# Summing the output's squares with a matrix of ones and taking the root for every column on GpSimd, in place of a root per token that is spread afterwards

## The chip, the core and the metric

The kernel runs on one core of a Trainium2 chip. The metric is the device time of one execution in microseconds (us); a kernel's time is the median of several runs. A profile of one further execution, taken by the hardware's own recorder, shows when each instruction ran. The engines are named as in the profile: PE is TensorE's matrix multiplication and PEld its loading of weights, DVE is VectorE, ACT is ScalarE, POOL is GpSimd, and SP is SyncE, which here only issues DMAs.

## The reference

One encoder layer is applied to 2,048 prompt tokens and 512 sample tokens of width 1,024 with shared weights. 16 learned meta tokens stand ahead of each sequence. The places that matter here are the last ones:

```python
y_a = (o_a * silu(za)) @ w_proj_a            # neighbourhood attention, gated
y_b = (o_b * silu(zb)) @ w_proj_b            # windowed attention, gated
h   = h + (sigmoid(ga) * y_a + sigmoid(gb) * y_b) @ w_out
out = h * rsqrt(mean(h * h, axis=-1) + 1e-6) * final_g      # the final RMSNorm
```

The final RMSNorm needs, for each token, the sum of squares over 1,024 features, its reciprocal root, and a product with all features of the token.

## The kernel before, in words

The 2,560 tokens are worked on in five windows of 512 (`NWIN`, `WTOK`), window 0 being the sample. Features lie on the 128 partitions and tokens along the free dimension, so that one row of features of a window is a tile of 128x512. All products run on pairs of tiles, a high part in `fp32r` and a low part that holds the rest of it, as three products (`mm3`, lines 146 to 148). The high part of a pair is a copy on ACT, the low part a subtraction; for weights (`wt`, `split_part`, lines 207 and 208) ACT copies and POOL subtracts, but for the last units of the last window, where `lo_eng` is DVE.

After the input projections, attention is cut into units: `unit_a` (neighbourhood) and `unit_b` (windowed), first all units "a" of a window, then all units "b". A hand-written loop interleaves the PE work of the units with a chain of generators called `dense`: at each place `fill` takes a few steps of it. PE's order is thus the order in which the code is written. ACT, DVE, POOL and, in this part, SP are ordered by a scheduler at build time; whatever order it chose, each engine and each queue then runs strictly in it.

For window w the dense chain is: `dense_pa(w)`, the product of `w_proj_a` with the gated output of branch a (PE tile `psa`, 8 rows of features, two steps each); `dense_pb(w)`, the same for branch b (`psb`); `dense_out(w)`, the product with `w_out` (`pso`). Those of neighbouring windows follow each other: units "b" of window w run beside the second half of `dense_out(w-1)` and `dense_pa(w)`, and units "a" of window w+1 beside `dense_pb(w)` and the first half of `dense_out(w)`.

`dense_out` leaves eight tiles `hT` (128x512, already multiplied by `final_g`), and POOL adds the squares of the features into one tile `ssq` (line 1372). `dense_fin(w-1)` runs in the steps of `dense_pa(w)` and closes window w-1. It sums `ssq` over the partitions by four products with a column of ones (`sums`, line 170: result `fin_v`, 128 tokens by 4), takes the reciprocal root of the 128x4 numbers on DVE (`rsqrt`, lines 153 to 163), puts them on diagonals (`diagonal`, line 177, tile `rs_dg`), spreads them to all partitions by four products with ones (`spread`, line 185, tile `rs_rb`), copies the result out of PSUM on ACT (`rbs`, line 1382), and multiplies the eight `hT` by it on POOL (line 1386). SP stores each. There are four such closings, of windows 0 to 3; the last window ends by other code (`finish_end`). They are called the first to the fourth closing here.

What else POOL does in that stretch matters: it makes the low parts of the weights (line 208), the gating product `y` of branch b (line 1280) and the low part `yb` of it (line 1072). The high part of `yb` is a copy on ACT (line 1071). `yb` has four parts, one for each pair of heads; the third and the fourth are made at the end of the units "b", and `dense_pb(w)` reads them as its third and fourth step of reduction for each row of features. In the fourth closing the third and fourth parts of `yb` are made on DVE instead.

PSUM tiles of the name `tp` (the transposes of probabilities, and `fin_v`, `rs_rb`) rotate over three banks.

Of the kernel before, what the change touches and what calls it, by code (L numbers as in the profile page):

```python
# [9 lines left out]
F32 = mybir.dt.float32  # L10
F32R = mybir.dt.float32r
I32 = mybir.dt.int32
AF = mybir.ActivationFunctionType
ALU = mybir.AluOpType
# [3 lines left out]
P = 128  # L18
D_MODEL = 1024
# [6 lines left out]
WTOK = 512  # L26
NWIN = TOK // WTOK
NEG = -1e30
EPS = 1e-6
# [66 lines left out]
def encoder_block(ctx: ExitStack, tc: tile.TileContext, xT, x_end, w_in, w_pa, w_pb, w_o, norm_g, final_g,  # L96
                  final_row, bias_a0, bias_a1, bias_a2, bias_a3, bias_b, bias_b0, outT_p, outT_s, out_e):
    nc = tc.nc
# [23 lines left out]
    def f32(ap):  # L122
        return ap.bitcast(F32)
# [17 lines left out]
    def move(out, in_):  # L141
        last_move[0] = nc.sync.dma_start(*(f32(a) if a.dtype == F32R else a for a in (out, in_)))
        return last_move[0]
# [6 lines left out]
    def rsqrt(small, sq, m, nc_):  # L150

        ve, hv, r, t = (small.tile([P, 8], F32, tag=f"rs{i}", name=f"rs{i}")[:m, :nc_] for i in range(4))
        nc.vector.tensor_scalar(ve, sq, 1.0 / D_MODEL, EPS, ALU.mult, ALU.add)
        nc.vector.tensor_scalar(r.bitcast(I32), ve.bitcast(I32), 1, None, ALU.arith_shift_right)
        nc.vector.tensor_scalar(r.bitcast(I32), r.bitcast(I32), -1.0, float(0x5F3759DF), ALU.mult, ALU.add)
        nc.vector.tensor_scalar(hv, ve, -0.5, None, ALU.mult)
        for _ in range(3):
            if nc_ == 1:
                nc.vector.scalar_tensor_tensor(t, r, hv, r, ALU.mult, ALU.mult)
            else:  # L160
                nc.vector.tensor_mul(t, r, hv)
                nc.vector.tensor_mul(t, t, r)
            nc.vector.scalar_tensor_tensor(r, t, 1.5, r, ALU.add, ALU.mult)
        return r

    def sums(ssq, c0, m, nc_, psum, tag):

        v = psum.tile([P, WTOK], F32, tag=tag, name="fin_v")
        for c in range(nc_):
            nc.tensor.matmul(v[:m, c : c + 1], ssq[:, c0 + c * m : c0 + (c + 1) * m], ones[:, 0:1],  # L170
                             start=True, stop=True)
        return v[:m, :nc_]

    def diagonal(dg, r, m, eng=nc.vector):

        nc_ = r.shape[1]
        eng.tensor_mul(dg[:m, : nc_ * m].rearrange("p (c n) -> p c n", n=m),
                             ident[:m, None, :m].broadcast_to([m, nc_, m]),
                             r[:m, :, None].broadcast_to([m, nc_, m]))

    def spread(psum, tag, dg, m, nc_):

        rb = psum.tile([P, WTOK], F32, tag=tag, name="rs_rb")
        for c in range(nc_):
            nc.tensor.matmul(rb[:, c * P : c * P + m], ones[:m, :], dg[:m, c * m : c * m + m], start=True, stop=True)
        return rb

    def by_ones(psum, tag, h, l, name):

        v = psum.tile([P, WTOK], F32, tag=tag, name=name)  # L190
        nc.tensor.matmul(v, ones_r, h, start=True, stop=False)
        nc.tensor.matmul(v, ones_r, l, start=False, stop=True)
        return v

    wpool = ctx.enter_context(tc.tile_pool(name="wpool", bufs=2))
    lo_eng, low = [nc.vector], [None]
# [1087 lines left out]
    pools = {}  # L1284
# [12 lines left out]
    acc = {}  # L1297
# [74 lines left out]
                nc.gpsimd.tensor_add(ssq, ssq, x)  # L1372

    def dense_fin(w):
        r = rsqrt(pools["d"], sums(acc["s", w], 0, P, 4, ps_p, "tp"), P, 4)
        dg = pools["d"].tile([P, WTOK], F32, tag="rbs", name="rs_dg", bufs=1)
        diagonal(dg, r, P)
        for _ in range(5):
            yield
        rb = spread(ps_p, "tp", dg, P, 4)  # L1380
        rbs = pools["d"].tile([P, WTOK], F32, tag="rbs", name="rbs", bufs=1)
        nc.scalar.copy(rbs, rb)
        for f in range(KT):
            hT = acc["h", w, f]
            with tc.issue_after(low[0]):
                nc.gpsimd.tensor_mul(hT, hT, rbs)
            dst = outT_s if w == 0 else outT_p
            c0 = 0 if w == 0 else (w - 1) * WTOK
            move(dst[f * P : (f + 1) * P, c0 : c0 + WTOK], hT)
            yield  # L1390
# [105 lines left out]
    def phases(w, br):  # L1496

        if br == "a":
            if w == 0:
                yield from islice(gates, GATES_A)  # L1500
            else:
                yield from dense_pb(w - 1)
                yield from dense_out(w - 1, range(0, 4))
        elif w == 0:
            yield from gates
            open_dense()
            yield from dense_pa(0)
        else:
            yield from dense_out(w - 1, range(4, 8))
            pa = dense_pa(w)  # L1510
            yield from islice(pa, 1)
            yield from with_fill(pa, dense_fin(w - 1))
# [8 lines left out]
    for w in range(NWIN):  # L1521
        for p in range(4):
            sh = {}
            units += [("a", w, unit_a(w, p, h, g, sh), 1) for h in range(2) for g in range(4)]
        for gh in range(2):
            sh = {}
# [15 lines left out]
    ps_p = ctx.enter_context(tc.tile_pool(name="ps_p", bufs=3, space=PSUM))  # L1542
# [9 lines left out]
    with tc.manual_schedule(engines={E.PE}):  # L1552
# [22 lines left out]
        for i in range(N):  # L1575
            br, w, _, weight = units[i]
# [128 lines left out]
```

## Time and profile before

| | |
|---|---|
| median of 3 runs | 1884.78 us (1884.11 to 1885.09) |
| profiled execution, its own time | 1881.95 us |
| its span, first to last instruction | 1880.0 us |
| granted TensorE clock | 0.998 |
| busy: PE, DVE, ACT, POOL | 1857.8, 1326.6, 1146.9, 729.4 us |

A row of the timeline reads: start in us from the span's start, duration in us, engine, line, operation, result<-operands, shapes and count; square brackets hold the idle time of the engine just before and what ended it. Consecutive instructions of one kind are merged into one row with their count. PE overlaps matrix products, so that the pitch, the distance between two starts, is what a product takes up and not its duration. A row of the groups ends in busy time, mean duration in ns, and idle time before.

### The profile page before, as it was taken

How to read it: one execution, taken by the hardware profiler on the slowest of the kernel's cores; microseconds unless marked ns; L12 is line 12 of the kernel's file. 1: busy time of each engine (PE TensorE's matmuls, PEld its weight loads, DVE VectorE, ACT ScalarE, POOL GpSimd, SP SyncE). 2: the span in 40 equal slices, each digit the busy share in tenths (PEclk: the TensorE clock that was granted, in tenths of full speed). 3: DMA queues.
4: the chain of work that ended last, by engine and by line, in shares of the span. 5: the costliest groups of instructions: out<-in, count | busy, mean ns of one | idle time of the engine just before them, and what ended most of it. 6: DMA issues, size and time to landing. Idle time of an engine off the chain costs nothing.

```text
span 1880.0 us, 29819 instructions
## 1 busy us (share of the span) xinstructions
PE 1857.8 (99%) x9797; PEld 1584.9 (84%) x9797; DVE 1326.6 (71%) x2961; ACT 1146.9 (61%) x2528; POOL 729.4 (39%) x558
## 2 busy tenths in 40 slices
PE   8999999999999999999999999999999999999998
PEld 6988888888888888888878888888888888888887
DVE  8885657556477565444457888878887887888874
ACT  6454444434465443444456797797889788878932
POOL 2005343222202322232323435656844764684420
PEclk9999999999999999999999999999999999999999
DMA  7575666555295677744359878977995996698473
GB/s 262 193 197 187 189 188 183 200 193 184 78 330 197 188 209 208 201 145 150 113 186 320 270 230 264 300 218 243 324 284 178 321 315 225 221 314 261 115 298 132
DMA packets 288145, 414.35 MB, mean 220 GB/s; under 512 B 117736, under 2 KB 162360, under 8 KB 286456
## 3 DMA queue, kind: packets, MB, share of 16 engines
q1 hardware_dynamic: 287704, 412.45, 68.4%
q8 instruction: 78, 1.28, 0.3%
q14 instruction: 75, 0.61, 0.1%
q10 hardware_dynamic: 288, 0.01, 0.0%
HBM read 303.46 MB, written 108.91 MB: 219 GB/s over the span
## 4 chain that ended last, share of the span: by engine, by line
PE 83%; ACT 5%; DVE 5%; DMA 4%; issue 1%; SPq 1%; POOL 1%; ACTq 0%; DVEq 0%
PE pa L850 23%; PE pe L850 11%; PE pc L850 6%; PE mm L148 3%; PE mm L147 3%; PE mm L146 3%; PE tp L1141 3%; PE pso L148 2%; PE psb L148 2%; PE pso L146 2%; PE psb L146 2%; PE pso L147 2%; PE psb L147 2%; PE psa L146 2%; PE psa L148 2%; PE psa L147 2%
## 5 line engine op out<-in xcount | busy, mean ns | idle before, releaser
L208 POOL TENSOR_TENSOR wt<-wraw,wt 128x512 fp32r<-128x512 f32 x164 | 213.0, 1317 | 270.0 <-ACT wt L207 269.9
L850 PE MATMUL pa<-u,wt 128*128 128x512 f32 x1008 | 244.3, 391 | 2.1 <-ACT wt L207 1.1
L850 PE MATMUL pa<-u,x 128*128 128x512 f32 x984 | 236.7, 389 | 0.5 <-ACT u L861 0.5
L850 PEld LDWEIGHTS pa<-u,wt 128*128 128x128 f32 x1008 | 189.9, 189 | 42.4 <-ACT wt L207 1.5
L207 ACT CAST wt<-wraw 128x512 fp32r<-128x512 f32 x312 | 177.9, 619 | 74.7 <-DMA wraw<-in_w_in_dram 27.4
L850 PEld LDWEIGHTS pa<-u,x 128*128 128x128 f32 x984 | 184.5, 188 | 39.3 <-ACT u L861 0.9
L821 POOL TENSOR_TENSOR s<-wraw,raw 128x512 f32<-128x512 f32 x40 | 58.2, 1456 | 278.8 <-DVE x L208 278.8
L146 PE MATMUL mm<-u,wt 128*128 128x512 f32 (+2 forms) x416 | 150.3, 361 | 7.0 <-ACT u L334 7.0
L816 POOL TENSOR_TENSOR s<-raw 128x512 f32<-128x512 f32 x40 | 58.7, 1467 | 234.7 <-DMA raw<-in_w_in_dram 233.2
L147 PE MATMUL mm<-u,wt 128*128 128x512 f32 (+2 forms) x416 | 146.8, 353 | 1.1 <-DVE u L335 1.0
L148 PE MATMUL mm<-u,wt 128*128 128x512 f32 (+2 forms) x416 | 146.8, 353 | 0.1
L208 DVE TENSOR_TENSOR wt<-wraw,wt 128x512 fp32r<-128x512 f32 x148 | 104.7, 745 | 53.8 <-ACT wt L207 53.7
L850 PE MATMUL pe<-u,wt 128*128 128x512 f32 x504 | 121.4, 390 | 0.0
L850 PE MATMUL pc<-u,wt 128*128 128x512 f32 x504 | 121.1, 389 | 0.0
L850 PE MATMUL pe<-u,x 128*128 128x512 f32 x480 | 115.3, 389 | 0.0
L850 PEld LDWEIGHTS pc<-u,wt 128*128 128x128 f32 x504 | 94.6, 188 | 19.6
L850 PEld LDWEIGHTS pe<-u,wt 128*128 128x128 f32 x504 | 94.4, 188 | 19.6
L1144 ACT CAST ph<-tp 128x384 fp32r<-128x384 f32 (+6 forms) x160 | 81.7, 511 | 44.9 <-PE tp L1141 43.5
L1047 DVE CUSTOM_DVE_ANT_0 s<-s,ba 128x384 f32<-128x384 f32 (+5 forms) x160 | 86.9, 544 | 30.6 <-PE s L1118 27.7
L1145 DVE TENSOR_TENSOR pl<-tp,ph 128x384 fp32r<-128x384 f32 (+6 forms) x160 | 94.9, 593 | 18.0 <-ACT ph L1144 15.2
L146 PE MATMUL pso<-mh,wt 128*128 128x512 f32 x256 | 107.1, 418 | 0.0
L829 POOL TENSOR_TENSOR s<-wraw,s 128x512 f32<-128x512 f32 x40 | 53.7, 1343 | 136.2 <-DVE wt L208 135.6
(258 smaller groups left out, 5030.1 us busy)
## 6 DMA issues: line engine op xcount, KB each, us to landing
wraw<-in_w_in_dram SPq DMA_DIRECT2D x86, 512.0 KB
raw<-in_w_in_dram SPq DMA_DIRECT2D x40, 512.0 KB
q<-qa SPq DMA_DIRECT2D x40, 512.0 KB
wraw<-in_w_o_dram SPq DMA_DIRECT2D x32, 512.0 KB
kbt<-kb SPq DMA_DIRECT2D x32, 384.0 KB
qa<-evq SPq DMA_DIRECT2D x20, 512.0 KB
qb<-evq SPq DMA_DIRECT2D x20, 512.0 KB
ka<-evk SPq DMA_DIRECT2D x20, 512.0 KB
```

Of the source, the lines that this page charges most:

```text
L146: nc.tensor.matmul(ps, wh, uh, start=first, stop=False)
L147: nc.tensor.matmul(ps, wh, ul, start=False, stop=False)
L148: nc.tensor.matmul(ps, wl, uh, start=False, stop=last)
L207: nc.scalar.copy(h, r)
L208: low[0] = (eng or lo_eng[0]).tensor_sub(l, r, f32(h)).ins
L816: eng.tensor_add(s1, a21, a22)
L821: eng.tensor_sub(s3, a11, a21)
L850: nc.tensor.matmul(ps, wt[:, a, s], u[:, b, kk, :], start=first and kk == 0 and i == 0, stop=kk == 3 and i == 2, skip_group_check=True)
L1047: nc.vector.tensor_tensor_reduce(s[:, :n], s[:, :n], bias, -1.0, 3.0e38, ALU.add, ALU.min, nm)
L1141: nc.tensor.transpose(tp[:kb, i * P : (i + 1) * P], pr[:, x : x + kb], ident)
L1144: nc.scalar.copy(ph_[:kb, a], tb)
L1145: nc.vector.tensor_sub(pl_[:kb, a], tb, f32(ph_[:kb, a]))
```

## The change

The sum over partitions is made for all 512 tokens at once and arrives on all 128 partitions. `ssq` is cut into a high part `ssh` (ACT) and a low part `ssl` (POOL), and two products of a 128x128 matrix of ones with them (`by_ones`, lines 191 and 192) give `fin_v`, 128x512, in which all partitions hold the same numbers. ACT copies it out of PSUM with scale and epsilon (`ve`), DVE makes a first guess of the reciprocal root from the bits in one instruction, and POOL takes three Newton steps of four instructions each on the full 128x512 tile. Nothing is put on a diagonal and nothing is spread. The tiles lie in the buffers of the low parts `ml` that are free at that time.

```diff
     def dense_fin(w):
-        r = rsqrt(pools["d"], sums(acc["s", w], 0, P, 4, ps_p, "tp"), P, 4)
-        dg = pools["d"].tile([P, WTOK], F32, tag="rbs", name="rs_dg", bufs=1)
-        diagonal(dg, r, P)
-        for _ in range(5):
+        ssq = acc["s", w]
+
+        def spare(i, dtype, name):
+            return pools["m"].tile([P, WTOK], dtype, tag=f"ml{i}", name=name)
+
+        sh, sl = (spare(i, F32R, f"ss{x}") for i, x in enumerate("hl"))
+        nc.scalar.copy(sh, ssq)
+        nc.gpsimd.tensor_sub(sl, ssq, f32(sh))
+        for _ in range(2):
             yield
-        rb = spread(ps_p, "tp", dg, P, 4)
-        rbs = pools["d"].tile([P, WTOK], F32, tag="rbs", name="rbs", bufs=1)
-        nc.scalar.copy(rbs, rb)
+        v = by_ones(ps_p, "tp", sh, sl, "fin_v")
+        ve, r, t = (spare(i, F32, name) for i, name in ((2, "ve"), (3, "rbs"), (4, "rt")))
+        nc.scalar.activation(ve, v, AF.Copy, bias=EPS, scale=1.0 / D_MODEL)
+        nc.vector.tensor_scalar(r.bitcast(I32), ve.bitcast(I32), -0.5, float(0x5F3759DF), ALU.mult, ALU.add)
+        for _ in range(3):
+            with tc.issue_after(low[0]):
+                nc.gpsimd.tensor_mul(t, r, ve)
+                nc.gpsimd.tensor_mul(t, t, r)
+                nc.gpsimd.tensor_scalar(t, t, -0.5, 1.5, ALU.mult, ALU.add)
+                nc.gpsimd.tensor_mul(r, r, t)
+            yield
         for f in range(KT):
             hT = acc["h", w, f]
             with tc.issue_after(low[0]):
-                nc.gpsimd.tensor_mul(hT, hT, rbs)
+                nc.gpsimd.tensor_mul(hT, hT, r)
```

`issue_after(low[0])` keeps an instruction behind the latest low part of weights in POOL's order. The scheduler's order moves with the change. On PE the first closing's sums stand behind a unit's transposes; before:

```order
L1243 MATMUL tp<-ident,prs 128x128 x6
L1246 MATMUL tp<-ident,prs 32x128
L170 MATMUL fin_v<-ones,ssq 128x1 x4
L146 MATMUL psa<-ya_11187,wt 128x512
L147 MATMUL psa<-ya_11188,wt 128x512
```

and now, one unit later:

```order
L1243 MATMUL tp<-ident,prs 128x128 x6
L1246 MATMUL tp<-ident,prs 32x128
L191 MATMUL fin_v<-ssh,ones 128x512
L192 MATMUL fin_v<-ssl,ones 128x512
L146 MATMUL psa<-ya_11187,wt 128x512
```

The sums moved behind the transposes of the next unit; the four products of line 185 are gone, and no other row of PE moved.

POOL, first closing, from the first `hT` on; `y_12477` and `y_12552` are the gating products of the third and fourth part of `yb_12614`. Before:

```order
L1386 TENSOR_TENSOR hT<-hT,rbs 128x512 x2
L208 TENSOR_TENSOR wt<-wraw,wt 128x512 x2
L1386 TENSOR_TENSOR hT<-hT,rbs 128x512 x4
L1280 TENSOR_TENSOR y_12477<-y_12477,z 128x512
L208 TENSOR_TENSOR wt<-wraw,wt 128x512 x2
L1386 TENSOR_TENSOR hT<-hT,rbs 128x512 x2
L1072 TENSOR_TENSOR yb_12614<-y_12477,yb_12613 128x512
L1280 TENSOR_TENSOR y_12552<-y_12552,z 128x512
L1072 TENSOR_TENSOR yb_12614<-y_12552,yb_12613 128x512
L208 TENSOR_TENSOR wt<-wraw,wt 128x512 x2
```

The same place now, from the third instruction of the second Newton step on (six instructions of the steps and two of line 208 stand ahead of these rows):

```order
L1393 TENSOR_SCALAR rt<-rt 128x512
L1394 TENSOR_TENSOR rbs<-rbs,rt 128x512
L1391 TENSOR_TENSOR rt<-rbs,ve 128x512
L1392 TENSOR_TENSOR rt<-rt,rbs 128x512
L1393 TENSOR_SCALAR rt<-rt 128x512
L1280 TENSOR_TENSOR y_12477<-y_12477,z 128x512
L1394 TENSOR_TENSOR rbs<-rbs,rt 128x512
L208 TENSOR_TENSOR wt<-wraw,wt 128x512 x2
L1399 TENSOR_TENSOR hT<-hT,rbs 128x512 x4
L1072 TENSOR_TENSOR yb_12614<-y_12477,yb_12613 128x512
L1399 TENSOR_TENSOR hT<-hT,rbs 128x512 x4
L1280 TENSOR_TENSOR y_12552<-y_12552,z 128x512
```

behind which come two of line 208 and then the last `yb_12614`. The gating product of the fourth part of `yb` now stands behind all Newton steps and all eight `hT`, and its low part behind two low parts of weights as well.

The second closing has the same order. In the third, POOL's end is:

```order
L1280 TENSOR_TENSOR y_17195<-y_17195,z 128x512
L1394 TENSOR_TENSOR rbs<-rbs,rt 128x512
L208 TENSOR_TENSOR wt<-wraw,wt 128x512 x2
L1072 TENSOR_TENSOR yb_17332<-y_17195,yb_17331 128x512
L1280 TENSOR_TENSOR y_17270<-y_17270,z 128x512
L1399 TENSOR_TENSOR hT<-hT,rbs 128x512 x8
L1072 TENSOR_TENSOR yb_17332<-y_17270,yb_17331 128x512
L208 TENSOR_TENSOR wt<-wraw,wt 128x512 x2
```

Here the gating product moved ahead of the `hT`, and only its low part, `yb`, stands behind all eight.

## The prediction

> **What bounds the kernel now.** I read the page's first part, then PE's waits in the last 680 us, where the closings lie, then the timelines of PE and POOL around each closing. The first row is from the page, the others are the whole answer on who made PE wait from 1200 us on (total, times, longest).
>
> ```profile
> PE 1857.8 (99%) x9797; PEld 1584.9 (84%) x9797; DVE 1326.6 (71%) x2961; ACT 1146.9 (61%) x2528; POOL 729.4 (39%) x558
> PE fin_v L170 <- DVE pms L1261: 0.5, 2, 0.3
> PE ob L1267 <- DVE y L1277: 0.5, 1, 0.5
> PE s L1223 <- DMA kbt<-kbm: 0.4, 1, 0.4
> PE fin_v L170 <- POOL ssq L1372: 0.3, 1, 0.3
> ```
>
> PE is the bound: it waits 1.7 us in 680. What leaves PE's order is gained, and any wait put into it is paid in full, since no idle time later can take it up. POOL's 39% is a mean; what counts is its queue in the closings.
>
> **What PE loses and gets.** First closing, PE's timeline: the sums, and the same passage one unit later without them.
>
> ```profile
> 1277.99 0.27 PE L1246 MATMUL tp<-ident,prs 128*32 128x128 f32 x1
> 1278.53 1.05 PE L170 MATMUL fin_v<-ones,ssq 128*128 128x1 f32 x8 [0.26 <-POOL ssq L1372]
> 1279.44 0.48 PE L146 MATMUL psa<-ya,wt 128*128 128x512 f32 x1
> 1279.76 0.40 PE L147 MATMUL psa<-ya,wt 128*128 128x512 f32 x1
> 1279.99 0.39 PE L148 MATMUL psa<-ya,wt 128*128 128x512 f32 x1
> ...
> 1284.49 0.27 PE L1246 MATMUL tp<-ident,prs 128*32 128x128 f32 x1
> 1284.52 0.49 PE L146 MATMUL psa<-ya,wt 128*128 128x512 f32 x1
> ```
>
> Without sums the next product starts 0.03 us after the transpose, with them 1.45 us after it: they cost 1.42. The fourth closing, where PE did not wait for them, and its spreading:
>
> ```profile
> 1778.04 0.27 PE L1246 MATMUL tp<-ident,prs 128*32 128x128 f32 x1
> ...
> 1779.24 0.48 PE L146 MATMUL psa<-ya,wt 128*128 128x512 f32 x1
> ...
> 1790.55 1.05 PE L185 MATMUL rs_rb<-rs_dg,ones 128*128 128x128 f32 x8
> 1791.36 0.48 PE L146 MATMUL psa<-ya,wt 128*128 128x512 f32 x1
> ```
>
> Sums 1.20 - 0.03 = 1.17; spreading 0.81. The four sums lie between 4 x 1.17 = 4.7 and 4 x 1.42 = 5.7; three of them had a wait of about 0.3, so I take 5.4. Spreading is 4 x 0.81 = 3.2. Added are two 128x512 products per closing at the pitch of lines 147 to 148 above, 0.23: 4 x 0.46 = 1.8. PE gains 5.4 + 3.2 - 1.8 = 6.8 us; up to the end of one of the first three closings it is ahead by 1.42 + 0.81 - 0.46 = 1.8.
>
> **What POOL gets.** Thirteen instructions on 128x512 per closing: `ssl`, nine two-input products and three of one input. First closing, before:
>
> ```profile
> 1284.73 2.54 POOL L208 TENSOR_TENSOR wt<-wraw,wt 128x512 fp32r<-128x512 f32 x2 [6.26 <-ACT wt L207]
> ...
> 1296.01 2.55 POOL L1386 TENSOR_TENSOR hT<-hT,rbs 128x512 f32<-128x512 f32 x2 [8.73 <-ACT rbs L1382]
> ...
> 1301.01 5.05 POOL L1386 TENSOR_TENSOR hT<-hT,rbs 128x512 f32<-128x512 f32 x4
> 1306.02 1.29 POOL L1280 TENSOR_TENSOR y<-y,z 128x512 f32<-128x512 f32 x1
> ...
> 1313.53 1.29 POOL L1280 TENSOR_TENSOR y<-y,z 128x512 f32<-128x512 f32 x1
> 1315.60 1.29 POOL L1072 TENSOR_TENSOR yb<-y,yb 128x512 fp32r<-128x512 f32 x1 [0.78 <-ACT yb L1071]
> 1316.84 2.55 POOL L208 TENSOR_TENSOR wt<-wraw,wt 128x512 fp32r<-128x512 f32 x2
> ```
>
> Idle for 6.26 and 8.73 us, then full. The last `yb` is done at 1316.9. PE's step that reads it is the fourth step of the first row of `dense_pb`; its second product (line 147) has the low part as operand:
>
> ```profile
> 1319.47 0.40 PE L146 MATMUL psb<-yb,wt 128*128 128x512 f32 x1
> 1319.71 0.39 PE L147 MATMUL psb<-yb,wt 128*128 128x512 f32 x1
> ```
>
> So `yb` had 2.8 us to spare, and PE will come 1.8 us earlier. Now this `yb` stands behind the whole of the Newton steps and the eight `hT`. Queued behind the slow POOL are ACT (the high part of `yb` needs the gating product) and PE.
>
> *Prices.* Mean of all `hT`, the only one-input instruction of this size, and two dependent POOL instructions at another place:
>
> ```profile
> L1386 POOL TENSOR_TENSOR hT<-hT,rbs 128x512 f32<-128x512 f32 x32 | 42.7, 1361 | 33.5 <-ACT rbs L1382 33.5
> L1370 POOL COPY ssq<-xres 128x512 f32<-128x512 f32 x4 | 2.5, 613 | 0.0
> 282.24 1.28 POOL L816 TENSOR_TENSOR s<-raw 128x512 f32<-128x512 f32 x1
> 283.60 1.62 POOL L817 TENSOR_TENSOR s<-s,wraw 128x512 f32<-128x512 f32 x1
> ```
>
> Independent two-input ones follow each other at (5.05 - 1.29) / 3 = 1.25 us at best and last 1.36 in the mean; I take 1.30. Dependent ones, as in a Newton step, came 283.60 - 282.24 = 1.36 apart; I take that, with 1.25 (the wait costs nothing) and 1.47 (1.36 and the mean's 0.11 more) as ends. The one-input TENSOR_SCALAR stands nowhere on POOL: at least the copy's 0.61, at most a two-input one's 1.47; nearest is the copy with one dependent wait of 0.11, 0.72. The Newton steps are 9 x 1.36 + 3 x 0.72 = 14.4 us (13.1 to 17.6).
>
> [...]
>
> *When the steps start.* The first guess needs PE's sums, then ACT and DVE. The transpose of 1284.49 comes at 1283.1; the two products end by 1283.8. ACT first does a unit's casts:
>
> ```profile
> 1285.65 0.86 ACT L1250 CAST ph<-tp 128x512 fp32r<-128x512 f32 x2
> 1295.35 0.58 ACT L1382 COPY rbs<-rs_rb 128x512 f32<-128x512 f32 x1
> ```
>
> If they move up with PE they end at about 1285.1, `ve` costs what `rbs` did, 0.6, and the guess on DVE about as much: 1286.4. POOL is free of line 208 by then (1287.3 - 1.4). For the second and third closing I take the end of that line's pair, less 1.4 (first and third row below: 1455.2 and 1622.2). A us earlier is the other end.
>
> ```profile
> 1453.49 3.09 POOL L208 TENSOR_TENSOR wt<-wraw,wt 128x512 fp32r<-128x512 f32 x2 [7.46 <-ACT wt L207]
> 1487.36 0.39 PE L147 MATMUL psb<-yb,wt 128*128 128x512 f32 x1
> 1620.50 3.09 POOL L208 TENSOR_TENSOR wt<-wraw,wt 128x512 fp32r<-128x512 f32 x2 [7.47 <-ACT wt L207]
> 1653.68 0.40 PE L147 MATMUL psb<-yb,wt 128*128 128x512 f32 x1
> ```
>
> *The sum.* From the start to the last `yb` POOL does, in the first two closings, the steps and 18 other two-input instructions: six low parts of weights, two gating products, two `yb`, eight `hT`. 14.4 + 18 x 1.30 = 37.8 (35.6 to 42.1). In the third the last two low parts come later: 16, and 35.2 (33.1 to 39.4). `yb` is ready at 1324.2, 1493.0 and 1657.4, where PE read it at 1319.7, 1487.4 and 1653.7. The difference is the net delay of the closing, PE's gain already inside, as it waits there anyway: +4.5 (1.3 to 8.8), +5.6 (2.4 to 9.9), +3.7 (0.6 to 7.9).
>
> Fourth closing: no `yb` on POOL, so the gain stays, -1.17 - 0.81 + 0.46 = -1.5. POOL's `hT` end later, and so do SP's stores, with loads of the tail behind them; DVE's two-input instructions are stretched while POOL runs:
>
> ```profile
> 1792.30 12.29 POOL L1386 TENSOR_TENSOR hT<-hT,rbs 128x512 f32<-128x512 f32 x8 [14.03 <-ACT rbs L1382]
> 1793.73 3.37 DVE L208 TENSOR_TENSOR wt<-wraw,wt 128x512 fp32r<-128x512 f32 x2
> 1815.66 0.92 SPq L142 DMA_DIRECT2D sgb<-gb  x2
> ```
>
> Steps from about 1786.5, 14.4 + 8 x 1.3: the `hT` end at 1811 instead of 1804.6, before the loads of 1815.66, which stand behind the last stores. For DVE's stretching I add 0.5 (0 to 3.5): -1.0 (-1.5 to +2.0).
>
> Costed at nothing: ACT's one more 128x512 instruction per closing (0.6), covered as PE waits for POOL afterwards; DVE's 13 small instructions and the diagonal, off PE's path. In the first closing the loads behind the stores of `hT` were issued about here:
>
> ```profile
> 1320.80 0.64 SPq L142 DMA_DIRECT2D q<-qa  x1
> ```
>
> The eighth `hT` ends at 1286.4 + 14.4 + 14 x 1.3 = 1319.0, so those loads keep their place, if barely.
>
> Total: 4.5 + 5.6 + 3.7 - 1.0 = +12.8 us (2.8 to 28.6) on the profiled execution, 1881.95 us, which lies 2.8 below the median of the runs. On that median, 1884.78: 1897.6 us, between 1887.6 and 1913.4.
>
> **The rivals.**
> - *`yb` comes in time* (faster). Then all of PE's gain stands: 1884.8 - 6.8 = 1878.0. From 1286.4 to where PE will read, 1319.7 - 1.8 = 1317.9, POOL has 31.5 us for 30 instructions, 1.05 each. It decides at that price; the two-input ones, 27 of the 30, never took under 1.25.
> - *Gain and wait cancel*: net delays below 1.3 us per closing, 1881 to 1888.6. It takes the lower ends of all prices and an early start.
> - *Longer still*: one-input instructions dearer than two-input ones, or DVE holding POOL up: beyond 28.6, over 1913. The copy's row speaks against the first.
> - *DVE held up rather than PE waiting for POOL.* DVE's normalisations of units "b" last 0.43 us, at worst 1.57:
>
> ```profile
> L1065 DVE TENSOR_SCALAR prs<-prs,rd x64: 360/431/1565, 1219.1 to 1784.5; 128x402 f32<-128x402 f32 x56, 128x274 f32<-128x274 f32 x8
> ```
>
> Three such DVE instructions per closing, each held 1.1 us, are 3.3 x 4 = 13.2 us less the 6.8: 1891. That wants `yb` in time as well, as the two waits overlap. [...]
>
> **How the numbers follow.** `yb` late by the prices above 0.68, longer still 0.07, DVE held up 0.05, cancelled 0.10, in time 0.10. A measurement of this kernel tells about 0.2%, 3.8 us, from no change. Slower is 0.68 + 0.07 + 0.05 = 0.80, same 0.10, faster 0.10. I predict the main case, 1898 us. The range 1886 to 1911 leaves out the faster case, half of the cancelled one and the longer one's far end.
>
> **What would show it.** Right: in the first three closings PE's waits name the third or fourth part of `yb` or its ACT copy at `psb`, some 4 to 9 us each, POOL has no gap from the first guess to the last `yb`, lines 191 and 192 pitch at 0.23. Wrong: `psb` starts without a wait; POOL's Newton steps take under 12 us; PE waits at `fin_v` for `ssl`, or at `tp`.

## The result, and the profile after

The changed kernel takes 1902.81 us (median of 5 runs, 1901.39 to 1904.55), the kernel before, measured beside it, 1884.11 (1883.30 to 1885.09): a ratio of 1.0101, 95% interval 1.0089 to 1.0113. It is slower by 1.0%, or 18.7 us. The prediction said slower, 1898 us, with a range of 1886 to 1911.

The profiled execution of the changed kernel has a span of 1900.6 us against 1880.0. The page's first part shows that PE is busy as before and that POOL has 61 us more:

```profile
PE 1859.1 (98%) x9741; PEld 1584.6 (83%) x9741; DVE 1321.1 (70%) x2909; ACT 1149.9 (60%) x2532; POOL 790.7 (42%) x610
```

What made PE wait from 1200 us on; where 1.7 us stood before, there are now 20.8:

```profile
PE psb L147 <- POOL yb L1072: 9.6, 3, 4.8
PE psb L146 <- ACT yb L1071: 7.7, 2, 3.9
PE pse L1459 <- DVE sgb L1444: 2.2, 1, 2.2
PE psb L146 <- DVE sgb L1444: 1.1, 1, 1.1
...
```

The three waits for POOL's `yb` and the two for ACT's copy of it lie in the first three closings. POOL's timeline in the first closing shows why. From the first Newton instruction to the last `yb` it has no gap, and the gating product of the fourth part (line 1280) comes only after all eight `hT`:

```profile
1286.00 1.28 POOL L1391 TENSOR_TENSOR rt<-rbs,ve 128x512 f32<-128x512 f32 x1 [1.57 <-DVE rbs L1388]
1287.37 1.30 POOL L1392 TENSOR_TENSOR rt<-rt,rbs 128x512 f32<-128x512 f32 x1
...
1306.54 5.04 POOL L1399 TENSOR_TENSOR hT<-hT,rbs 128x512 f32<-128x512 f32 x4
...
1312.77 5.01 POOL L1399 TENSOR_TENSOR hT<-hT,rbs 128x512 f32<-128x512 f32 x4
1317.72 1.28 POOL L1280 TENSOR_TENSOR y<-y,z 128x512 f32<-128x512 f32 x1
...
1321.39 1.28 POOL L1072 TENSOR_TENSOR yb<-y,yb 128x512 fp32r<-128x512 f32 x1
```

PE at the same place: the new products with ones, then the two waits, and behind them something that the prediction did not have. Line 148 used to start 0.23 us after line 147; here products of this size follow each other at about 0.43:

```profile
1281.18 0.27 PE L1246 MATMUL tp<-ident,prs 128*32 128x128 f32 x1
1281.27 0.47 PE L191 MATMUL fin_v<-ssh,ones 128*128 128x512 f32 x1
1281.58 0.40 PE L192 MATMUL fin_v<-ssl,ones 128*128 128x512 f32 x1
1281.81 0.40 PE L146 MATMUL psa<-ya,wt 128*128 128x512 f32 x1
...
1319.70 0.79 PE L146 MATMUL psb<-yb,wt 128*128 128x512 f32 x1 [3.85 <-ACT yb L1071]
1322.72 0.80 PE L147 MATMUL psb<-yb,wt 128*128 128x512 f32 x1 [2.23 <-POOL yb L1072]
...
1326.73 0.63 PE L147 MATMUL psb<-yb,wt 128*128 128x512 f32 x1
1327.16 0.63 PE L148 MATMUL psb<-yb,wt 128*128 128x512 f32 x1
```

The table of windows names the reason. A row holds a stretch and its length, the busy time and number of instructions of PE, PEld, DVE, ACT and POOL, and then the granted clock, the DMA share and GB/s. The clock falls to half at 1318.05, while PE waits, and comes back at 1328.29, 5.6 us after PE has its operand:

```profile
1314.64:1318.05 3.41, 1.21 (x8) 0.74 (x6) 2.56 (x8) 1.16 (x3) 3.41 (x4) 1.00 1.08 326
1318.05:1321.47 3.42, 0.79 (x1) 0.29 (x1) 0.00 (x0) 0.62 (x1) 3.42 (x4) 0.50 1.03 306
...
1324.88:1328.29 3.41, 3.41 (x11) 2.72 (x11) 1.48 (x4) 2.00 (x5) 2.42 (x2) 0.50 1.01 396
1328.29:1331.71 3.42, 3.42 (x22) 2.94 (x22) 1.67 (x5) 1.85 (x5) 0.00 (x0) 1.00 0.64 236
```

The other two closings look alike:

```profile
1497.21 0.79 PE L147 MATMUL psb<-yb,wt 128*128 128x512 f32 x1 [2.52 <-POOL yb L1072]
...
1668.99 0.79 PE L147 MATMUL psb<-yb,wt 128*128 128x512 f32 x1 [4.82 <-POOL yb L1072]
```

To see where the time went, one product is followed through both traces: the first `psa` of each `dense_pa`, which stands just ahead of each closing. Before, for the second to fourth closing, and a transpose behind the fourth:

```profile
1440.60 0.48 PE L146 MATMUL psa<-ya,wt 128*128 128x512 f32 x1
1607.60 0.48 PE L146 MATMUL psa<-ya,wt 128*128 128x512 f32 x1
1773.18 0.49 PE L146 MATMUL psa<-ya,wt 128*128 128x512 f32 x1
1793.27 0.27 PE L1246 MATMUL tp<-ident,prs 128*32 128x128 f32 x1
```

and after:

```profile
1445.47 0.48 PE L146 MATMUL psa<-ya,wt 128*128 128x512 f32 x1
1619.77 0.48 PE L146 MATMUL psa<-ya,wt 128*128 128x512 f32 x1
1790.45 0.49 PE L146 MATMUL psa<-ya,wt 128*128 128x512 f32 x1
1809.04 0.27 PE L1246 MATMUL tp<-ident,prs 128*32 128x128 f32 x1
```

The delay is 4.87, 12.17, 17.27 and 15.77 us at these places. At the landmark ahead of the first closing (1273.14 and 1271.27) it is -1.87, by which the one execution happens to be ahead; in the experiments below this product lies anywhere between 1270.3 and 1274.0. So the first three closings cost 6.7, 7.3 and 5.1 us, the fourth gains 1.5, and from there to the end of the span another 4.8 us are lost (20.6 - 15.8).

### The profile page after: what moved, and what is told of

It is laid out like the page before. It is cut to its first block, busy times and chain, and to the rows that moved or that the text cites. A ratio compares the mean times of both kernels' runs of the same rounds, so it can differ in the third digit from the quotient of the medians.

```text
span 1900.6 us, 29716 instructions
## 1 busy us (share of the span) xinstructions
PE 1859.1 (98%) x9741; PEld 1584.6 (83%) x9741; DVE 1321.1 (70%) x2909; ACT 1149.9 (60%) x2532; POOL 790.7 (42%) x610
## 3 DMA queue, kind: packets, MB, share of 16 engines
q8 instruction: 78, 1.28, 0.3%
## 4 chain that ended last, share of the span: by engine, by line
PE 75%; ACT 5%; POOL 4%; DVE 4%; DMA 3%; issue 2%; SPq 0%; POOLq 0%; DVEq 0%; ACTq 0%
PE pa L850 23%; PE pe L850 12%; PE pc L850 6%; PE tp L1141 3%; PE mm L148 2%; PE mm L146 2%; PE mm L147 2%; PE pso L148 2%; PE pso L146 2%; PE pso L147 2%; PE psb L147 2%; PE oa L1158 2%; PE oa L1156 2%; POOL hT L1399 2%; PE psb L148 2%
```

## The experiments

Eleven kernels were run. Each ratio below is to the kernel before, measured beside that run (medians of 1884.6 to 1885.9 us). The expectations speak of 8.1 us of half clock in the three closings and of 2.1 us that PE gains in the fourth. That came from transposes of the two traces that had been paired wrongly; by the `psa` rows above it is 6.1 and 1.5 (worked out in the section on the prediction).

**PE's part of the change alone.** The twelve instructions of the Newton steps are gone, the rest stays:

```diff
         for _ in range(3):
-            with tc.issue_after(low[0]):
-                nc.gpsimd.tensor_mul(t, r, ve)
-                ...
             yield
```

> The changed kernel without the twelve POOL instructions of the Newton steps; they are left out, so the hT are multiplied by the rough first guess. POOL's order is then that of the kernel before, but for the one subtraction ssl, and PE has the products with ones. Theory (PE's part is a gain, and all the loss comes from POOL's steps): no wait at psb, no late sgb in the tail, the whole of PE's gain: 1884 - 6.8 = 1877 to 1878. Rival (the products with ones, ACT's or DVE's new instructions bring waits of their own): 1882 or more.

Measured: 1876.56 us, ratio to before 0.9948 (0.9934 to 0.9962). From 1195 us on PE waits 2.0 us in all, for `kbt`, `kd` and `pr` and for none of the tiles of the change. The largest group is

```profile
PE s L1223 <- DMA kbt<-kbm: 1.3, 2, 0.7
```

Dropping the spreading is the gain that the prediction worked out, and all of the loss comes with the steps on POOL. Each of the following kernels tries to keep the one without the other.

**Does the half clock follow from the wait?** Work is added to PE where it would wait:

```diff
+            if f == 0 and 1 <= w <= 3:
+                for _ in range(22):
+                    nc.tensor.matmul(ps, ones_r, yh[:, 0, :], start=True, stop=True)
             for k in range(4):
```

> The changed kernel with work added on PE: in windows 1 to 3, 22 products of 128x512 with ones ahead of the first row of dense_pb, 22 x 0.23 = 5.1 us, whose result is overwritten. They lie where PE would otherwise wait 6.1, 6.4 and 4.8 us. Theory (half clock follows from the idle time): the waits shrink to 1.0, 1.3 and 0, the clock stays full, and the kernel gets faster by the 8.1 us of half clock, less 0.3 in the third closing: 1895. Rival one (the slow clock at that place has another cause, such as the work that stands there): no change, 1903. Rival two (PE does not have the time to spare, and the products cost what they last): 1902.8 + 15.2 = 1918.

Measured: 1896.54 us, ratio to before 1.0056 (1.0038 to 1.0074), so 6 us less than the changed kernel. With 15 us of work more, the kernel got faster. The waits for `yb` shrank to two of 1.6 us, and the clock stayed full behind them; first the row of the waits, then the window behind the first of them:

```profile
PE psb L147 <- POOL yb L1072: 3.2, 2, 1.6
```

```profile
1326.00:1330.00 4.00, 4.00 (x23) 3.33 (x22) 2.54 (x7) 3.60 (x8) 2.01 (x2) 1.00 1.02 399
```

By the `psa` rows of this trace the first three closings cost 4.3, 5.0 and 3.4 us instead of 6.7, 7.3 and 5.1. Both rivals fall: the slow clock is a price of the wait itself.

**Less on POOL.** Two steps instead of three:

```diff
-        for _ in range(3):
+        for _ in range(2):
```

> The changed kernel with two Newton steps on POOL instead of three; the third step's accuracy is left out. Theory (POOL makes the last parts of yb late, PE waits for them, and PE runs at half clock for some us behind such a wait): one step is 3 x 1.37 + 0.65 = 4.8 us of POOL. PE's waits at psb, 6.1, 6.4 and 4.8 us in the first three closings, become 1.3, 1.6 and 0, and the half clock, 8.1 us in sum, goes with them: 1902.8 - 14.4 - 8.1 = 1880, down to 1876 if the tail gains as well. Rival one (the clock has nothing to do with the wait): 1902.8 - 14.4 = 1888. Rival two (DVE is held up by POOL's instructions and that is what costs): a third of the added POOL time gone gives a third of the 18.7 us, 1897. Rival three (the products with ones or ACT's work cost it): 1903.

Measured: 1888.22 us, ratio 1.0009 (0.9999 to 1.0019). This is rival one's number, but not by its reason. The waits are 7.0 us and not 2.9 (the order changed too: in the first closing seven `hT` now stand ahead of the third part's gating product), and two waits for DMAs, 2.0 us, came in; in the tail PE waits 2.3 us for `sgb`. Half clock followed one of the three waits in the closings, not the others (the product behind the wait lasts 0.80 or 0.5 us); the last section has the idle times of PE there:

```profile
1318.90 0.80 PE L147 MATMUL psb<-yb,wt 128*128 128x512 f32 x1 [2.17 <-POOL yb L1072]
1487.75 0.51 PE L147 MATMUL psb<-yb,wt 128*128 128x512 f32 x1 [2.13 <-DVE pr L1065]
1657.73 0.50 PE L147 MATMUL psb<-yb,wt 128*128 128x512 f32 x1 [2.74 <-POOL yb L1072]
```

**The last parts of `yb` taken off POOL:**

```diff
-            eng = nc.vector if w == NWIN - 1 and gh else nc.gpsimd
+            eng = nc.vector if gh else nc.gpsimd
```

> The changed kernel, with the gating products and the low parts of the third and fourth part of yb on DVE in all windows, as the last window has them; POOL keeps the three Newton steps and the hT. Theory (the queue ahead of yb on POOL is the cause): no wait at psb, full clock in the closings, so 17.3 us of waits and 8.1 us of half clock go: 1902.8 - 25.4 = 1877, the late sgb of the tail still inside; up to 1880 if DVE comes a little late. Rival one (DVE, held up by POOL, is what costs; it now gets four more instructions of 0.7 to 1.8 us per closing): 1903 or more. Rival two (the late hT and their stores, or the low parts of weights behind them, hold PE up): 1895 or more, with PE waiting for wt or a DMA.

Measured: 1887.88 us, ratio 1.0016 (1.0004 to 1.0027). No wait at `psb` for `yb` is left, which is the theory's part of it; 15 us of the loss go. Of what is left, the tail's waits for `sgb` (2.9 us) stand as expected, and 7.3 us are rival one's mechanism at a smaller price than it named: DVE's gating products last longer while POOL runs (two of the ten ran with POOL idle and took 0.67 and 0.68 us; of the eight beside POOL seven took 0.88 to 1.37), and PE waits for the probabilities that stand behind them. The row of the waits, and the group of the gating products with minimum, median and maximum in ns:

```profile
PE tp L1141 <- DVE pr L1065: 7.3, 7, 1.3
```

```profile
L1280 DVE TENSOR_TENSOR y<-y,z x10: 670/948/1367, 1143.4 to 1804.3; 128x512 f32<-128x512 f32 x10
```

**The same work on POOL in another order.** The loop of the `hT` becomes a generator of its own, `scaled`, that runs beside `dense_pb`, and the root gets a buffer that lives that long:

```diff
+                    yield from islice(pb, 2)
+                    pb = with_fill(pb, scaled(w - 2, acc["r", w - 2]))
```

> The changed kernel with the same instructions in another order: in the first three closings the eight hT products on POOL (and their stores) come in the steps of dense_pb, behind the last yb, instead of ahead of it. The fourth closing stays. Theory (only the queue ahead of yb counts, not POOL's load): POOL has 8 x 1.25 = 10 us less ahead of the last yb, which was late by 6.1 us at most; no wait at psb, full clock: 1902.8 - 17.3 - 8.1 = 1877, the tail's loss of some 5 us still inside. [...] Rival two (the hT come to stand in the way of the gating sums and low parts of dense_pb): PE waits at psb for DVE or at pso, 1890 or more.

Measured: 1887.77 us, ratio 1.0015 (1.0006 to 1.0025). PE's whole order, the Newton steps and the `hT` are those of the changed kernel, POOL is as busy (792.0 us against 790.7), and no wait for `yb` is left: it was the queue ahead of `yb`. But the `hT` now stand ahead of the sums and low parts of `dense_pb`, rival two, at 5.6 us:

```profile
PE pso L146 <- DVE sgb L1345: 4.0, 2, 2.2
...
PE pso L147 <- POOL ml L1350: 1.6, 4, 0.6
```

**The Newton steps on DVE:**

```diff
-                nc.gpsimd.tensor_mul(t, r, ve)
+            nc.vector.tensor_mul(t, r, ve)
                 ...
```

> The changed kernel with the twelve instructions of the Newton steps on DVE instead of POOL; the products with ones stay, nothing is spread. It shows what PE's part of the change is worth. Theory: POOL's queue is as before and yb in time, so the waits at psb and the tail's late loads go. If DVE has the room for 12 x 0.7 = 8 us per closing, PE's gain of 6.8 us stands: 1884 - 6.8 = 1877. Since the gating products alone on DVE made PE wait 7.3 us for it (pr), I expect waits for DVE at tp instead, 1 to 4 us per closing: 1880 to 1893. Rival (the products with ones themselves cost PE time): above 1893 without a wait for DVE.

Measured: 1913.62 us, ratio 1.0152 (1.0133 to 1.0171), beyond both expectations. I had counted DVE's time and not its queue. A chain of twelve dependent instructions, each behind other work, ran from 1287.4 to 1310.0 in the first closing. POOL stood idle for 9.4 us, as DVE's part of the third gating product came late, and then its order was fixed: the `hT`, ready to go only now, ahead of the fourth gating product. `yb` was later than ever:

```profile
1306.18 1.30 POOL L1280 TENSOR_TENSOR y<-y,z 128x512 f32<-128x512 f32 x1 [9.39 <-DVE y L1277]
...
1311.15 5.04 POOL L1398 TENSOR_TENSOR hT<-hT,rbs 128x512 f32<-128x512 f32 x4
...
1326.06 1.30 POOL L1072 TENSOR_TENSOR yb<-y,yb 128x512 fp32r<-128x512 f32 x1
```

**POOL's load on the kernel before.** The small roots and the spreading stay, the same steps run on POOL beside them:

```diff
+                nc.gpsimd.tensor_mul(t, rr, ve)
+                ...
+                nc.gpsimd.tensor_mul(rr, rbs if i == 2 else rr, t)
```

> The kernel before (sums per token and spreading stay on PE, the small roots on DVE) with the same 13 instructions on POOL per closing, on the sums per partition instead of the total, which need not wait for PE; hT is multiplied by the spread root times the last factor of these steps, about 1. The steps can start some 2 to 3 us earlier than in the changed kernel. Theory (POOL's load alone is enough): the last yb is late by 11.7 us in sum as in the changed kernel, less 2 to 3 us for each of three closings, so 3 to 6 us, with half clock 0 to 8 us and the tail 5 us: 1884 + 8 to 19 = 1892 to 1903. Rival (the products with ones on PE, or ACT's and DVE's new instructions, cost the time): 1884 to 1888.

Measured: 1918.78 us, ratio 1.0174 (1.0156 to 1.0192). This missed, and it isn't the clean test it was meant to be: PE waits 27.5 us from 1200 on, 24.9 of them for DVE. DVE's small instructions of the old root, 128x4, stand in the same stretch as POOL's steps and last longer there, 0.85 us in the mean instead of 0.51. Line 163 by groups between 1276 and 1300, before and here:

```profile
L163 DVE SCALAR_TENSOR_TENSOR rs<-rs,rs 128x4 f32<-128x4 f32 x3 | 1.5, 514 | 0.1
```

```profile
L163 DVE SCALAR_TENSOR_TENSOR rs<-rs,rs 128x4 f32<-128x4 f32 x3 | 2.5, 845 | 0.0
```

It shows the prediction's fourth rival at work. In the closings of the changed kernel, where those small instructions are gone, PE waits for DVE nowhere.

**The tail.** The fourth closing as in the kernel before, the first three changed:

```diff
     def dense_fin(w):
+        if w == NWIN - 2:
+            r = rsqrt(pools["d"], sums(acc["s", w], 0, P, 4, ps_p, "tp"), P, 4)
+            ...
+            return
```

> The changed kernel with the fourth closing as in the kernel before (sums per token, small roots on DVE, spreading); the first three stay changed. It tells what the fourth closing costs with the tail behind it: by the landmarks of the two traces PE gains 2.1 us in it and loses 4.8 in the tail. Theory: the late sgb of the tail go, 1902.8 - 2.7 = 1900. Rival (the tail is late whatever the fourth closing does, because the third is late): 1902.8 + 2.1 = 1905.

Measured: 1900.12 us, ratio 1.0073 (1.0059 to 1.0086): 2.7 us less than the changed kernel, as expected, and no wait in the tail. (From the landmark ahead of the fourth closing to the end, the changed kernel loses 3.4 us on the kernel before, 20.6 - 17.3, and this one nothing.) So the fourth closing alone causes the late tail. By what path was tried by moving its stores to POOL's queue:

```diff
-            move(dst[...], hT)
+            if w == NWIN - 2:
+                nc.gpsimd.dma_start(dst[...], hT)
+            else:
+                move(dst[...], hT)
```

> The changed kernel with the eight stores of the fourth closing issued on POOL's own DMA queue instead of SP's; everything else as it is. Theory for the tail (SP waits for the late hT, and the loads of sgb that stand behind the stores land late): the waits at psb and pse for DVE sgb, 3.5 us, and the half clock behind them go, some 4 to 5 us: 1898. Rival (in the tail it is DVE, stretched by POOL's hT, that comes late): DVE still ends its sgb late, 1902 to 1903.

Measured: 1902.14 us, ratio 1.0093 (1.0070 to 1.0117), no change. The waits for `sgb` fell from 3.3 to 0.2 us, but DVE waits for a later pair of them, and PE for the `mh` made from it. From the waits and DVE's timeline:

```profile
PE pse L1462 <- ACT mh L1451: 2.4, 2, 1.6
```

```profile
1853.44 0.69 DVE L1447 TENSOR_TENSOR sgb<-psb,sgb 128x512 f32<-128x512 f32 x1 [4.16 <-DMA sgb<-gb]
```

The DMA share is 0.99 to 1.04 from 1824 to 1860 here: with the stores on another queue the DMA engines are as full as without. The windows of the other two traces show what the late `hT` did. First the kernel before, then the changed one at about the same place of PE's order:

```profile
1800.00:1806.00 6.00, 6.00 (x27) 4.58 (x26) 5.87 (x10) 2.66 (x5) 4.60 (x3) 1.00 0.69 260
```

```profile
1818.00:1824.00 6.00, 6.00 (x28) 4.96 (x27) 6.00 (x8) 1.77 (x3) 5.84 (x5) 1.00 0.22 85
```

Before, the eight stores are issued from 1793.6 to 1806.3, while the DMA engines have room (a share of 0.45 to 0.84 from 1788 to 1812), ahead of a stretch at a full share (1.00 to 1.03 from 1812 to 1842). In the changed kernel that room is left unused (0.00 from 1816 to 1822), and the stores, issued from 1822.9 to 1837, fall into the full stretch (1.01 to 1.04 from 1824 to 1860). Eight times 256 KB at its some 410 GB/s take 5.1 us, an estimate from these rows, where the tail lost 4.8. That this is the whole cause is argued from these rows, not shown.

Both edits together, late `hT` and the other queue:

> Both of the above together: hT behind the last yb in the first three closings, and the fourth closing's stores on POOL's queue. Theory: PE's gain alone is left, no wait and no half clock: 1884 - 6.8 - some 1 to 3 that this kernel is earlier before the closings = 1874 to 1878, faster than both kernels. If the tail's loss has another cause than the stores, 1877 to 1882. Rival (POOL's load as such costs): 1890 or more.

Measured: 1889.29 us, ratio 1.0022 (1.0011 to 1.0032), like the late `hT` alone; the waits at `pso` (4.6 us) and for `mh` (2.4 us) are both there.

**A version meant to keep the gain.** The `hT` come one at a time, every fourth step, in `dense_pb` and then `dense_out`; the fourth closing is the old one:

```diff
+    def beside(main, extra):
+        for i, _ in enumerate(main):
+            yield
+            if i % 4 == 0:
+                next(extra, None)
...
+                yield from beside(pb, sc)
+                yield from beside(dense_out(w - 1, range(0, 4)), sc)
```

> A version meant to keep PE's gain: in the first three closings the hT come one by one behind the last yb, four in dense_pb and four in dense_out (all eight in dense_pb made PE wait 5.6 us at pso, behind DVE's and POOL's work on sgb and ml); the fourth closing as in the kernel before. Theory: no wait at psb, at most 1 us at pso, no late sgb in the tail: PE's gain of the first three closings stands, 3 x 1.8 = 5.4, so 1884 - 5.4 = 1879. Rival one (POOL has no room for the steps anywhere near: the wait only moves on): 1884 to 1888. Rival two (the late stores hold up loads on SP's queue): a wait for a DMA, 1882 to 1890.

Measured: 1881.68 us, ratio 0.9979 (0.9968 to 0.9991). It is faster than both kernels, by a little. No wait for `yb`, at `pso` or in the tail is left; the largest of its five remaining groups is

```profile
PE s L1223 <- DMA kbt<-kbm: 0.8, 1, 0.8
```

and the sum of all five is 3.2 us, where the kernel before has 1.7. PE gains 1.9 us in each of the first three closings, where 1.8 was worked out. Behind the first it then loses 1.3 us of that, and behind the second 2.6, in pieces of under 1 us; the kernel without Newton steps loses 1.2 and 0.8 at these places. Which of them the late `hT` cause was not tried.

## Why the prediction was right, and where its sum fell short

The main mechanism held at every point that it named but one, the pitch of lines 191 and 192 (below): waits at `psb` in the first three closings of 6.1, 6.4 and 4.8 us (4 to 9 were named), no gap on POOL, no wait at `fin_v` or `tp`. Term by term, with the position of PE where it reads the last `yb`, less the delay at the landmark ahead:

| step | predicted | measured |
|---|---|---|
| one dependent two-input instruction | 1.36 | 1.37 (1287.37 - 1286.00) |
| an independent one | 1.30 | 1.25 ((5.04 - 1.28) / 3) |
| start of the steps, three closings | 1286.4, 1455.2, 1622.2 | 1287.9, 1455.6, 1622.6 (1286.00 + 1.87, 1460.44 - 4.87, 1634.72 - 12.17) |
| start to last `yb`, first closing | 37.8 | 36.7 (1286.00 to 1322.67) |
| late `yb`, first closing | +4.5 | +4.9 (1322.72 + 1.87 - 1319.71) |
| second | +5.6 | +5.0 (1497.21 - 4.87 - 1487.36) |
| third | +3.7 | +3.1 (1668.99 - 12.17 - 1653.68) |
| PE's gain in the fourth closing | -1.5 | -1.5 (15.77 - 17.27) |
| half clock behind the waits, net | not in the sum | +1.9, +2.3, +2.0 (the closing's 6.7, 7.3, 5.1 less the late `yb`) |
| tail | +0.5 | +4.8 |

The three waits came to 13.0 us where 13.8 were predicted. Two steps of the sum failed.

The first is the sentence that the difference "is the net delay of the closing". It took a wait as costing its own length. PE comes out of it at half clock, which adds 6.1 us net in the three closings. Followed product by product through both traces, the delay grows from 3.0, 9.9 and 15.3 us at the last `yb` to 5.7, 12.3 and 17.3 once the clock is full, 7.1 in sum; 0.7 comes back at one place where the kernel before waits for a DMA (1380.97) and the changed one does not. The added work on PE took back 6.3 us of 1902.8 and so confirms the size. How long PE had been idle ahead of half clock is in the last section.

The second is the tail, where the prediction has the `hT` ending "at 1811 instead of 1804.6, before the loads of 1815.66". On that axis they ended at 1818.3:

```profile
1803.93 1.28 POOL L1391 TENSOR_TENSOR rt<-rbs,ve 128x512 f32<-128x512 f32 x1 [5.53 <-DVE rbs L1388]
...
1818.65 1.78 POOL L1394 TENSOR_TENSOR rbs<-rbs,rt 128x512 f32<-128x512 f32 x1
1820.51 13.61 POOL L1399 TENSOR_TENSOR hT<-hT,rbs 128x512 f32<-128x512 f32 x8
```

The steps started 1.7 us later than assumed (1803.93 - 15.77 = 1788.2 against 1786.5) and took 16.6 us instead of 14.4, the `hT` 13.6 instead of 10.4. In the last window DVE makes low parts of weights and of `yb`, and beside these, instructions of both engines are longer: on POOL up to 1.78 us instead of 1.28, on DVE 1.77 for the `yb` of 1820.91, where a gating product of that size takes 0.67 with POOL idle (in the run with the last parts of `yb` on DVE). The prediction gave this stretching to DVE alone, though its own row of `hT` before (12.29 us for eight) showed it on POOL.

The smaller term: the two products with ones cost 0.6 us of PE per closing (1281.81 - 1281.18, less 0.03), not 0.46, as the first starts 0.09 after the transpose and has a pitch of 0.31. Against that, the kernel without Newton steps gained 8 to 10 us where 6.8 were predicted, and its trace shows 1.9 us for each of the first three closings (1.8 were predicted), so PE's part was if anything undervalued. In sum 13.0 + 6.1 - 1.5 + 4.8 = 22.4 us from the first closing on, in these two executions; the one after was 1.9 ahead by then, and the one before lies 2.2 below its median, so that the medians differ by 18.7 where the prediction had 12.8. That 1902.8 lies in the range all the same is in part luck: the range reached to 1911 for dearer instructions on POOL, which did not come, and that room was taken by the half clock, which was not in the sum, and by the tail, which cost 4.8 where at most 3.5 was allowed.

## What to carry to other kernels

Before work is moved to an engine with a low share of busy time, its queue in that stretch is to be written out up to the next tile that the bound engine reads: here 37 us of work stood ahead of one low part, and the order, not the load, made the loss. Where PE is made to wait, the clock behind the wait is to be looked at too: here half clock came with the waits of 6.1, 6.4 and 4.8 us and cost some 2 us of PE for each closing, and behind two waits of 1.6 us (added work on PE) the clock stayed full. And where an early end lets transfers run ahead of a tail, work out the end with the slowest rows of that stretch, not with the mean.

## What the runs showed of the hardware

In the traces of the kernels before and after, all stretches at half clock begin at multiples of 3.41 us from one another: at 131.16 and 1875.38 us before, at 1318.05, 1495.55, 1666.21, 1847.12 and 1894.91 us after. Those that begin before PE's last product last 3.41, 6.83 or 10.24 us. Cut into windows of that length at these places, the two traces have, from 1200 us to PE's last product, 390 windows at full clock. The four in which PE was idle for 2.92, 2.20, 2.05 and 1.99 us were followed by half clock, the 386 with 1.80 us or less were not. Of the eight windows at half clock the four with at most 0.18 us of idle time led back to full clock, and the four with 1.26 us or more did not. Ahead of 1200 us, a window with 1.79 us of idle time, from 127.75 in the kernel before, was followed by half clock as well. (Ends of PE's products are modelled, so these idle times are rough.) The run with two Newton steps has two waits of nearly one length, 2.17 and 2.13 us. They leave 1.96 and 1.81 us of idle time in one window, and only behind the first is the clock of the next one half:

```profile
1315.27:1318.69 3.42, 1.46 (x9) 0.94 (x7) 3.38 (x9) 1.83 (x6) 3.42 (x3) 1.00 1.08 338
1318.69:1322.10 3.41, 3.19 (x12) 2.70 (x13) 0.86 (x3) 0.00 (x0) 1.33 (x2) 0.50 1.06 280
...
1485.94:1489.35 3.41, 1.60 (x10) 1.41 (x11) 2.42 (x5) 0.67 (x2) 1.81 (x3) 1.00 1.06 238
1489.35:1492.77 3.42, 3.42 (x21) 2.92 (x20) 1.99 (x5) 2.54 (x6) 2.19 (x2) 1.00 1.05 322
```

Its wait of 2.74 us, from 1654.99 to 1657.73, is spread over two windows, 1.61 and 1.13 us (1318.69 + 99 x 3.4133 = 1656.6 lies between), and the product behind it lasts 0.50 us, as at full clock. One of 1.82 us, with late `hT` at the first `pso`, ends at 1358.18 and is followed by half clock: the mean clock is 0.96 from 1356 to 1360, 0.61 to 1364 and 1.00 to 1368, which makes some 3.4 us at half clock that begin some 1.5 us after PE has gone on, an estimate from these three.

GpSimd's TENSOR_SCALAR on 128x512 lasted between 0.61 us (first closing) and 0.94 (fourth, beside DVE's low parts); its two-input instructions went from 1.28 to 1.78 there. VectorE's line 163 on 128x4 took 0.16 us with POOL idle (1282.13, kernel before) and 1.22 beside POOL's low parts of weights (1286.08). In these rows an instruction's size alone does not give its duration.
